# Two transformer blocks on one core: SBUF laid out anew, with stage boundaries and the routing reordered

## The chip, the core and the metric

The kernel runs on one core of one Trainium2 chip as a single program: TensorE (PE) multiplies matrices, VectorE (DVE), ScalarE (ACT) and GpSimd (POOL) do the rest, SyncE (SP) issues most DMA transfers. Everything on chip lives in SBUF (128 partitions; addresses below are offsets within a partition) or in the eight banks of PSUM, into which PE writes. The metric is the device time of one execution in microseconds (us); the median of three runs stands for the kernel.

## The reference

The input is 512 tokens of 1024 float32 values. Two layers of a first block are followed by one second block:

```python
for l in range(2):                              # first block
    h = rms_norm(x, attn_norm[l])
    proj = h @ w_in[l]                          # 13 parts: fox q k v f, diff q k v, dsa q k v, index q k w
    o = concat(fox_attention, diff_attention, dsa_attention)   # dsa: top 128 keys chosen by the index scores
    x = x + o @ w_out[l]
    gate, up = split(rms_norm(x, ffn_norm[l]) @ w_gate_up[l])  # 1024 -> 2 x 2816
    x = x + (silu(gate) * up) @ w_down[l]
proj = rms_norm_2(x, mix_norm_gain) @ w_in_2    # second block: q, k, v, u, two gates
merged = gate0 * (chunked_attention(q, k, v) @ wb[:512]) + gate1 * (s5_ssm_glu(u) @ wb[512:])
x = x + merged @ w_out_2
h = rms_norm_2(x, ffn_norm_gain_2)
x = x + moe(h)       # 4 groups of 4 experts, 1024 -> 256 -> 1024; the best group, 2 experts of it per token
```

## The kernel before

**Precision.** A float32 product is made of three reduced ones. `unit` fetches 4 KiB per partition of weights (`raw`, DMA issued by SP, L158), ACT rounds them to `hi` (L162), and DVE or POOL forms the rest `lo` (L164). An activation matrix is kept the same way, transposed, as `Th` and `Tl` (two tiles each, for k 0 to 3 and 4 to 7): `put_T` transposes one block of 128 tokens and 512 features on PE (L196), ACT copies it to Th (L199), DVE writes the rest to Tl (L200). The product is three matmuls: `mm3` (L174 to L176) moves weights against stationary activations, `mm3w` (L1139 to L1141) moves activations against stationary weights. In the profile `out<-moving,stationary` names the operands; s, f, t and o are the PSUM banks, two of each, s and f for accumulators.

**Order.** The program is written engine-free; a scheduler sets each engine's order from the order of the code, the buffers and their releases. Every tile that is reused waits for its last reader.

**Stages.** A norm is opened (`norm_open`), fed a block at a time (`norm_block`: DVE multiplies by the gain into `big`, L217, `put_T`, ACT sums squares, L219) and closed (`norm_close`, L223 to L226, gives the factor r per token, which is applied after the products). Each mixer closes the norm, then `project` makes the index, key and value part (4 accumulators over 8 k's); from these banks qk_norm (L289 to L297, its reciprocal root at L134 to L141), the v split (L372) and per block z, ix and iw (L575 to L577) read directly. A second projection follows, then attention in softmax passes: scores on PE, maximum m on DVE, exponential p on ACT (L428), halves pp on ACT and POOL (L433), transposed pt. Then the product with w_out feeds the FFN's norm. The FFN works column by column: gate and up by `mm3w` (t and o), then the down products by `mm3` (s and f) from the rounded hidden halves hh and hl.

**Second block.** u is projected for each of four token phases (slice r of stride 4). Its factor per phase, r4, is made by writing r to a DRAM row rd and reading it back in another order (L976, L978). `ssm` copies the banks out as um with it (L1409). The attention's and SSM's outputs are yA and yS; branch products and gates give `merged` (mh, ml), which w_out takes. In its last half each block's eight k's give 20 logits by `mm3` (96 matmuls of 20 columns over the four blocks); then lg (L1542), ranks, the list of slots, and a gather per expert from the normalised copy hd (stored at L1606 after normalisation on ACT, L1605). The gather buffers xe are zeroed first by POOL (L1680). Sixteen experts follow, each with six units of weights.

**Where things lie** (built addresses, KiB): hi 33.8 to 45.8, lo 45.8 to 57.8, Th and Tl of mixers and second block 57.8 to 90, yA and yS 108 to 138, hh and hl 108 to 160, the FFN's Th and Tl in a pool of their own (`home`) at 190 to 222, expert weights' spare hi and lo at 184 to 208.

## Time and profile before

| | us |
|---|---|
| median of 3 runs (1992.2, 2000.2, 2000.66) | 2000.2 |
| the profiled execution | 2000.87 |
| its span on the core | 1999.1 |
| PE busy in the span | 1852.3 |
| DVE, ACT, POOL busy | 1244.6, 871.2, 532.4 |

| stage | us from the span's start |
|---|---|
| load and first norm | 0 to 30 |
| mixer, FFN (layer 0) | 30 to 338, 338 to 720 |
| mixer, FFN (layer 1) | 733 to 1010, 1030 to 1406 |
| second block to w_out | 1407 to 1777 |
| routing, MoE, end | 1777 to 1812, to 1966, to 1999 |

The profiled execution took 1.8 us more than its span. "Busy" of PE counts pipelined matmuls whose records overlap, so a matmul's cost is read from start to start. The granted clock of PE is a share of full speed: 1.00 is 2.4 GHz, 0.50 is 1.2 GHz.

### The profile page before, as it was taken

How to read it: one execution, taken by the hardware profiler on the slowest of the kernel's cores; microseconds unless marked ns; L12 is line 12 of the kernel's file. 1: busy time of each engine (PE TensorE's matmuls, PEld its weight loads, DVE VectorE, ACT ScalarE, POOL GpSimd, SP SyncE). 2: the span in 40 equal slices, each digit the busy share in tenths (PEclk: the TensorE clock that was granted, in tenths of full speed). 3: DMA queues.
4: the chain of work that ended last, by engine and by line, in shares of the span. 5: the costliest groups of instructions: out<-in, count | busy, mean ns of one | idle time of the engine just before them, and what ended most of it. 6: DMA issues, size and time to landing. Idle time of an engine off the chain costs nothing.

```text
span 1999.1 us, 30880 instructions
## 1 busy us (share of the span) xinstructions
PE 1852.3 (93%) x11506; PEld 1552.9 (78%) x11506; DVE 1244.6 (62%) x2779; ACT 871.2 (44%) x1411; POOL 532.4 (27%) x452
## 2 busy tenths in 40 slices
PE   6998798999999999978999999999899989997994
PEld 5788687888888878867978888888788778886783
DVE  4789875433334458998776687534265465457994
ACT  4455564322122234555652222323234674345883
POOL 4476640000000045765300000000344640022321
PEclk8999899999999999999999999999899999988997
DMA  5244764333333242556744355332642455567993
GB/s 160 56 101 100 149 115 118 95 95 95 95 95 95 85 127 75 109 113 136 137 117 110 110 169 154 114 112 85 223 148 64 106 125 160 195 245 253 309 308 65
DMA packets 383890, 265.88 MB, mean 133 GB/s; under 512 B 163713, under 2 KB 344989, under 8 KB 383217
## 3 DMA queue, kind: packets, MB, share of 16 engines
q1 hardware_dynamic: 379120, 255.39, 46.3%
q0 software_dynamic: 4608, 8.40, 1.8%
q8 instruction: 93, 1.52, 0.3%
q14 instruction: 69, 0.56, 0.1%
HBM read 213.21 MB, written 26.26 MB: 120 GB/s over the span
## 4 chain that ended last, share of the span: by engine, by line
PE 65%; DVE 16%; DMA 10%; issue 4%; ACT 3%; POOL 2%; SPq 0%; POOLq 0%; ACTq 0%; DVEq 0%
PE f L174 5%; PE f L175 5%; PE f L176 5%; PE t L1139 4%; PE t L1140 4%; PE t L1141 4%; PE o L1139 4%; PE s L174 4%; PE o L1140 4%; PE o L1141 4%; PE s L175 4%; PE s L176 4%; DVE lo L164 2%; DVE m L608 2%; DVE work L609 2%
## 5 line engine op out<-in xcount | busy, mean ns | idle before, releaser
L162 ACT CAST hi<-raw 128x1024 fp32r<-128x1024 f32 (+2 forms) x330 | 334.2, 1017 | 681.7 <-PE f L176 233.1
L164 POOL TENSOR_TENSOR lo<-raw,hi 128x1024 fp32r<-128x1024 f32 (+1 forms) x89 | 205.7, 2316 | 673.7 <-ACT hi L162 673.5
L164 DVE TENSOR_TENSOR lo<-raw,hi 128x1024 fp32r<-128x1024 f32 (+1 forms) x241 | 287.2, 1200 | 146.1 <-ACT hi L162 135.3
L174 PE MATMUL f<-hi,Th 128*128 128x256 f32 (+2 forms) x800 | 257.4, 322 | 6.9 <-DVE vt L372 4.3
L175 PE MATMUL f<-lo,Th 128*128 128x256 f32 (+2 forms) x800 | 256.3, 320 | 0.5 <-POOL lo L164 0.5
L176 PE MATMUL f<-hi,Tl 128*128 128x256 f32 (+2 forms) x800 | 255.3, 319 | 0.3 <-DVE m L426 0.3
L174 PEld LDWEIGHTS f<-hi,Th 128*128 128x128 f32 x800 | 157.5, 197 | 17.4 <-issue 2.9
L175 PEld LDWEIGHTS f<-lo,Th 128*128 128x128 f32 x800 | 157.9, 197 | 8.7 <-POOL lo L164 1.0
L176 PEld LDWEIGHTS f<-hi,Tl 128*128 128x128 f32 x800 | 157.2, 197 | 8.7 <-DVE m L426 0.7
L1139 PE MATMUL t<-Th,hi 128*128 128x512 f32 x352 | 140.5, 399 | 0.0
L1140 PE MATMUL t<-Tl,hi 128*128 128x512 f32 x352 | 139.8, 397 | 0.0
L1141 PE MATMUL t<-Th,lo 128*128 128x512 f32 x352 | 139.6, 397 | 0.0
L1139 PE MATMUL o<-Th,hi 128*128 128x512 f32 x352 | 139.1, 395 | 0.0
L1141 PE MATMUL o<-Th,lo 128*128 128x512 f32 x352 | 138.9, 395 | 0.0
L1140 PE MATMUL o<-Tl,hi 128*128 128x512 f32 x352 | 138.9, 395 | 0.0
L174 PE MATMUL s<-hi,Th 128*128 128x512 f32 (+1 forms) x224 | 92.4, 413 | 18.2 <-ACT um L1409 8.5
L433 POOL TENSOR_TENSOR pp<-p,pp 128x384 f16<-128x384 f32 (+1 forms) x82 | 80.8, 991 | 90.8 <-ACT pp L432 74.4
L428 ACT ACTIVATE p<-p,m 128x384 f32<-128x384 f32 (+3 forms) x128 | 67.5, 557 | 68.1 <-DVE m L426 53.8
L175 PE MATMUL s<-lo,Th 128*128 128x512 f32 (+1 forms) x224 | 91.4, 408 | 3.2 <-POOL lo L164 3.2
L176 PE MATMUL s<-hi,Tl 128*128 128x512 f32 (+1 forms) x224 | 90.9, 406 | 0.0
L174 PE MATMUL f<-hi,hh 128*128 128x512 f32 x208 | 82.8, 398 | 2.7 <-ACT hh L1784 2.2
L176 PE MATMUL f<-hi,hl 128*128 128x512 f32 x208 | 82.6, 398 | 0.6 <-DVE hl L1785 0.6
(735 smaller groups left out, 4742.0 us busy)
## 6 DMA issues: line engine op xcount, KB each, us to landing
raw<-in_w_gate_up_dram SPq DMA_DIRECT2D x88, 512.0 KB, 3.9
raw<-in_w_in_dram SPq DMA_DIRECT2D x52, 512.0 KB, 4.0
raw<-in_w_down_dram SPq DMA_DIRECT2D x44, 512.0 KB, 3.7
raw<-in_w_e_down_dram SPq DMA_DIRECT2D x26, 512.0 KB, 8.3
raw<-in_w_e_gate_dram SPq DMA_DIRECT2D x50, 256.0 KB, 7.2
raw<-in_w_e_up_dram SPq DMA_DIRECT2D x50, 256.0 KB, 7.2
par<-par SPq DMA_DIRECT2D x4, 2304.0 KB, 11.5
raw<-in_w_in_dram SPq DMA_DIRECT2D x32, 256.0 KB, 3.2
```

Of the source, the lines that this page charges most:

```text
L162: nc.scalar.copy(hi, raw)
L164: low.tensor_tensor(out=lo, in0=raw, in1=hi.bitcast(F32), op=ALU.subtract)
L174: nc.tensor.matmul(out, l[0], r[0], start=start, stop=False)
L175: nc.tensor.matmul(out, l[0], r[1], start=False, stop=False)
L176: nc.tensor.matmul(out, l[1], r[0], start=False, stop=stop)
L428: nc.scalar.activation(p[:, at[qb]:at[qb] + (qb + 1) * P], src[qb], AF.Exp, bias=m[:, i:i + 1], scale=-1.0)
L433: nc.gpsimd.tensor_tensor(out=pp[:, o:2 * o], in0=p[:, :o], in1=pp[:, :o], op=ALU.subtract)
L608: nc.vector.max(m8, work[qb])
L609: nc.vector.match_replace(out=work[qb], in_to_replace=m8, in_values=work[qb], imm_value=TAKEN)
L1139: nc.tensor.matmul(out, w[0], r[0], start=start, stop=False)
L1140: nc.tensor.matmul(out, w[0], r[1], start=False, stop=False)
L1141: nc.tensor.matmul(out, w[1], r[0], start=False, stop=stop)
```

## The change

**Layout.** The pool of hi and lo now lies lowest (hi 16 to 28, lo 28 to 40), and above it eight slabs of 8 KiB, two sets of four (40 to 72 and 72 to 104). A norm's T takes one set: the FFN's set 1, the others' set 0. The set not in use serves as room: the mixer's softmax buffers (`KINDS`: s for p, p for pp, t for pt) and the relu of the index scores, yA and yS, um and U, the spare hi and lo of the experts. raw, big and constants lie above 104; hh and hl at 140 to 187, mh and ml at 172 to 204.

**Boundaries.** `norm_block` puts its transposes on a list, and `flush(n, 1)` runs them a block late; the last ones are flushed after the first four k's of the next stage's first product, in `project`, in the FFN's first column and in `logits`. `norm_close` follows that product. In the mixer's start every accumulator is copied out once (p0, in `big`), and qk_norm, v, z, ix and iw read p0. In the second block r4 is made from the broadcast row of r by a masked sum, and um is copied by ACT and DVE in turn.

**Routing.** `logits` takes the 40 columns of router weights (hi and lo side by side) as the stationary operand and moves T (384, then 128 tokens), then copies and transposes the result. hd is stored unnormalised, a block at a time during w_out, as is the output; r goes into the gates. The memsets are gone. Between the halves of w_out expert 0's gate and up units are fetched and split. hi and lo have 7 sets in place of 6; weights wait in 20 raw buffers by turns in place of 23, after a first few.

```diff
-SLOTS = {'p': 2, 'pp': 2, 'pt': 5}
...
-PRE = 15
+PRE = 7
...
-MORE_D, MORE_F = ('sp', 'ttpptt')
+KINDS, MORE_F = 'sssppptttttt', 'tttp'
...
+        self.ring = pool("ring", bufs=3)
+        self.hp = pool("hp", bufs=1)
+        self.cur = 0
...
+        self.rawp = pool("rawp", bufs=3)
+        self.bigp = pool("bigp", bufs=1)
...
-        hi = ring.tile([P, n], F32R, tag="hi", name="hi")
-        lo = ring.tile([P, n], F32R, tag="lo", name="lo")
+        hi, lo = (next(self.rings) if self.rings else self.parts_of(self.ring))(n)
...
+        return self.bigp.tile([P, NT, D], F32, tag="big", name="big", bufs=1)
+
+    def slab(self, k, dt=F32R, other=True):
+
+        return self.hp.tile([P, 4, S], dt, tag=f"T{self.cur ^ other}{k}", name=f"T{k}")
+
+    def new_T(self, other=False):
+        self.cur ^= other
+        return [[self.slab(2 * j + i, other=False) for i in range(2)] for j in range(2)]
...
-        self.put_T(n.T, n.big[:, tb, :], tb, h)
+        n.todo.append(lambda: self.put_T(n.T, n.big[:, tb, :], tb, h))
         nc.scalar.activation(self.junk, n.x[tb][:, hs], AF.Square, accum_out=n.ss[:, h, tb:tb + 1])
+
+    @staticmethod
+    def flush(n, left=0):
+
+        while len(n.todo) > left:
+            n.todo.pop(0)()
...
                 done([b.rearrange("p (t c) -> p t c", t=2) for b in banks])
             yield
 
-    def project(self, T, w, parts, order=range(KD // 2)):
+    def project(self, T, w, parts, sl=lambda tb: slice(tb * P, (tb + 1) * P), norm=None):
+
         acc = [self.acc() for _ in range(NT)]
         n = sum(n for _, n in parts)
-        for i, k2 in enumerate(order):
-            hi, lo = self.columns(w, (2 * k2, 2 * k2 + 1), parts)
-            for kk in range(2):
-                for tb in range(NT):
-                    self.mm3(acc[tb][:, :n], self.Tk(T, 2 * k2 + kk, slice(tb * P, (tb + 1) * P)), (hi[:, kk, :], lo[:, kk, :]), i == kk == 0, i == KD // 2 - 1 and kk == 1)
+        for h in range(2):
+            units = []
+            for k2 in (2 * h, 2 * h + 1):
+                hi, lo = self.columns(w, (2 * k2, 2 * k2 + 1), parts)
+                units += [(2 * k2 + kk, hi[:, kk, :], lo[:, kk, :]) for kk in range(2)]
+                if norm is None or h:
+                    for k, hi, lo in units:
+                        for tb in range(NT):
+                            self.mm3(acc[tb][:, :n], self.Tk(T, k, sl(tb)), (hi, lo), k == 0, k == KD - 1)
+                    units = []
+            for tb in range(NT):
+                for k, hi, lo in units:
+                    self.mm3(acc[tb][:, :n], self.Tk(T, k, sl(tb)), (hi, lo), k == 0, False)
+            if norm is not None and h == 0:
+                self.flush(norm)
         return acc
 
...
+                    self.flush(n, 1)
...
+        acc = self.project(T, w, [(SK, IW + 4 - SK), (FF, 6)], norm=n)
+        self.norm_close(n)
+        p0 = self.big()[:, :, 0:IW + 10 - SK]
+        for tb in range(NT):
+            r = rx[:, tb:tb + 1]
+            if tb % 2:
+                nc.vector.tensor_scalar(p0[:, tb, :], acc[tb][:, 0:IW + 10 - SK], r, None, op0=ALU.mult)
+            else:
+                nc.scalar.activation(p0[:, tb, :], acc[tb][:, 0:IW + 10 - SK], AF.Copy, scale=r)
...
+        room = [v[:, i * S:(i + 1) * S] for v in slabs[0:3] for i in range(4)]
         sqk = one.tile([P, NT, 7 * 64], F32, name="sqk")
-        r_sk = self.qk_norm(acc, 0, 1, 64, g_sk, sqk[:, :, 384:448], "sk", ex)
-        sv = self.v_parts(acc, SV - SK, 1, "sv", rx)
...
-        for tb in range(NT):
-            r = rx[:, tb:tb + 1]
-            nc.vector.scalar_tensor_tensor(z[:, tb, :], acc[tb][:, IW + 4 - SK:IW + 10 - SK], r, fb, op0=ALU.mult, op1=ALU.add)
-            nc.scalar.activation(ix[:, tb, :], acc[tb][:, IQ - SK:IW - SK], AF.Copy, scale=r)
-            nc.vector.tensor_scalar(iw[:, tb, :], acc[tb][:, IW - SK:IW - SK + 4], r, 0.5, op0=ALU.mult, op1=ALU.mult)
-        ixv = ix.rearrange("p t (h d) -> p t h d", h=5)
...
-                rl = self.att.tile([P, S], F32, tag="p", name="rl", bufs=SLOTS["p"])[:, :L]
+                rl = next(rls)[:, :L]
...
                         self.norm_block(following, tb, half)
+                        self.flush(following, 1)
...
+                        self.flush(n)
                     if c == 0:
+                        self.norm_close(n)
...
-        rd = self.dram.tile([S], F32, name="rd")
-        nc.sync.dma_start(out=rd.rearrange("(t p) -> p t", p=P), in_=rx)
-        r4 = self.tiny.tile([P, 4], F32, name="r4")
-        nc.sync.dma_start(out=r4, in_=rd.rearrange("(m r) -> m r", r=4))
...
-        yS = [(ys.tile([P, S], F32R, name=f"ysh{i}"), ys.tile([P, S], F32R, name=f"ysl{i}")) for i in range(4)]
+        pairs = lambda h, l: [(h[:, i, :], l[:, i, :]) for i in range(4)]
+        yS = pairs(self.slab(0), self.slab(2))
...
+                acc = self.project(T, w, [(1536, 512)], lambda r: slice(r, S, 4), n)
+                self.norm_close(n)
+                self.norm_row(n, self.raw_of(self.rawp)(S), self.upto)
+
+                r4, t4 = self.tiny.tile([P, 4], F32, name="r4"), self.raw_of(self.rawp)(S).rearrange("p (r m) -> p r m", r=4)
+                nc.vector.tensor_mul(t4, n.rB.rearrange("p (m r) -> p r m", r=4), self.ident[:, None, :].to_broadcast([P, 4, P]))
+                nc.vector.tensor_reduce(r4, t4, axis=AX.X, op=ALU.add)
...
+            self.hd = self.dram.tile([S, D], F32, name="hd")
             self.pre = self.ctx.enter_context(tc.tile_pool(name="pre", bufs=PRE))
+
+            sets = [[self.slab(k) for k in (j, j + 2)] for j in range(2)]
+            self.sets = [lambda n, h=h, l=l, i=i: [v[:, i:i + 2, :].rearrange("p a t -> p (a t)")[:, 0:n] for v in (h, l)] for h, l in sets for i in (0, 2)]
...
                     if half:
-                        for k in range(KD):
-                            self.mm3(self.logits[:, tb * 20:(tb + 1) * 20], self.Tk(n.T, k, slice(tb * P, (tb + 1) * P)), (self.rw[0][:, k, :], self.rw[1][:, k, :]), k == 0, k == KD - 1)
+                        nc.sync.dma_start(out=self.hd[tb * P:(tb + 1) * P, :], in_=n.big[:, tb, :])
+                        nc.sync.dma_start(out=out[tb * P:(tb + 1) * P, :], in_=x[tb])
+                    self.flush(n, 1)
                 return add
 
             for half in range(2):
                 self.accumulate(put(half), half, wo, [(k, 2) for k in range(0, KD, 2)], lambda k, t: (M[k][0][:, t], M[k][1][:, t]), half)
+                if half == 0:
+                    self.raws, self.rings = cycle([self.raw_of(self.pre)]), iter(self.sets)
+                    self.ahead = list(gate_up(self, 0))
+                    self.raws = self.rings = None
+            self.norm_close(n)
+            logits(self, n)
...
     for r in range(4):
-        nc.scalar.activation(um[:, :, r, :], acc[r].rearrange("p (g c) -> p g c", g=NG), AF.Copy, scale=r4[:, r:r + 1])
+        src = acc[r].rearrange("p (g c) -> p g c", g=NG)
+        if r % 2:
+            E.tensor_scalar(um[:, :, r, :], src, r4[:, r:r + 1], None, op0=ALU.mult)
+        else:
+            nc.scalar.activation(um[:, :, r, :], src, AF.Copy, scale=r4[:, r:r + 1])
...
-    self.logits = self.sm()
+
+    self.rw = c.tile([P, KD, 40], F32R, name="rwp")
+    nc.scalar.copy(self.rw[:, :, 0:20], raw)
+    nc.vector.tensor_sub(self.rw[:, :, 20:40], raw, self.rw[:, :, 0:20].bitcast(F32))
+    self.lb = self.sm()
+
+
+def logits(self, n):
+
+
+    nc = self.nc
+    ps = self.lb
+
+    def add(ks, c0, c1):
+        for k in ks:
+            hi, lo = self.Tk(n.T, k, slice(c0, c1))
+            mm = [(40, hi), (20, lo)]
+            for m, v in mm[::-1] if k == KD - 1 else mm:
+                nc.tensor.matmul(ps[0:m, c0:c1], self.rw[:, k, 0:m], v, start=k == 0 and m == 40, stop=k == KD - 1 and m == 40)
+
+    last = S - P
+    add(range(KD), 0, last)
+    add(range(4), last, S)
+    self.flush(n)
+    add(range(4, KD), last, S)
+    lT = self.raw_of(self.rawp)(S)
+    nc.scalar.copy(lT[0:40, 0:256], ps[0:40, 0:256])
+    nc.vector.tensor_copy(lT[0:40, 256:S], ps[0:40, 256:S])
+    ps = self.sm()
+    for tb in range(NT):
+        nc.tensor.transpose(ps[:, tb * 40:(tb + 1) * 40], lT[0:40, tb * P:(tb + 1) * P], self.ident[0:40, 0:40])
+    self.logits = ps[:, 0:NT * 40].rearrange("p (t c) -> p t c", t=NT)
 
...
-    for tb in range(NT):
-        E.scalar_tensor_tensor(lg[:, tb].rearrange("p g e -> p (g e)"), self.logits[:, tb * 20:(tb + 1) * 20], n.r[:, tb:tb + 1], self.rb, op0=ALU.mult, op1=ALU.add)
+    lf = lg.rearrange("p t g e -> p t (g e)")
+    E.tensor_copy(lf, self.logits[:, :, 20:40])
+    E.tensor_add(lf, lf, self.logits[:, :, 0:20])
+    E.tensor_mul(lf, lf, n.r[:, :, None].to_broadcast([P, NT, 20]))
+    E.tensor_add(lf, lf, self.rb[:, None, :].to_broadcast([P, NT, 20]))
...
-        for tb in range(NT):
-            nc.scalar.activation(n.big[:, tb, :], n.big[:, tb, :], AF.Copy, scale=n.r[:, tb:tb + 1])
-            nc.sync.dma_start(out=hd[tb * P:(tb + 1) * P, :], in_=n.big[:, tb, :])
-        self.store_x(x, out)
...
+        self.rings = cycle([ring, sets[0], sets[1], ring, sets[2], sets[3], ring])
+        self.raws = chain([self.raw_of(self.pre)] * (PRE - 4), cycle([self.raw_of(self.pre)] * 4 + [self.raw_of(self.rawp)] * 3 + [self.raw_of(self.more)] * MORE + [lambda n, v=v: v[:, 0:n] for v in x[XR:] + room] + [self.raw_of(self.pre)] * (PRE - 4)))
...
-        for v in xe:
-            nc.gpsimd.memset(v, 0.0)
...
-    for k, w in gate_up(self, e):
+    ahead, self.ahead = self.ahead, None
+    for k, w in ahead or gate_up(self, e):
         self.mm3(ps, (xh[:, k], xl[:, k]), w, k == 0, k == KD - 1)
```

PE at the first mixer's end and the FFN's start, before (big is the normed block, t and o banks; L196 transposes):

```order
L176 MATMUL f<-hi,Tl 128x512
L196 MATMUL t<-ident,big 128x128 x4
L196 MATMUL o<-ident,big 128x128 x4
L196 MATMUL t<-ident,big 128x128 x4
L196 MATMUL o<-ident,big 128x128 x4
L1139 MATMUL t<-Th,hi 128x512
L1140 MATMUL t<-Tl,hi 128x512
L1141 MATMUL t<-Th,lo 128x512
```

The same place after (T_4380 and T_4382 are Th and Tl for k 0 to 3, T_4381 is Th for k 4 to 7; L202 transposes):

```order
L180 MATMUL f<-hi,T_2613 128x512
L202 MATMUL t<-ident,big 128x128 x4
L202 MATMUL o<-ident,big 128x128 x4
L1182 MATMUL o<-T_4380,hi 128x512
L1183 MATMUL o<-T_4382,hi 128x512
L1184 MATMUL o<-T_4380,lo 128x512
...
L202 MATMUL t<-ident,big 128x128 x4
L1182 MATMUL t<-T_4380,hi 128x512
...
L202 MATMUL o<-ident,big 128x128 x4
L248 MATMUL t<-big,ones 128x128 x2
L1182 MATMUL o<-T_4381,hi 128x512
```

Two of the four groups of transposes now stand behind 12 and 24 gate or up products of the first four k's.

SP's queue at the second block's start, before (rd and r are the factor on its way, bias and rel the attention's, raw weights):

```order
L976 DMA rd<-n_14336 128x4x1
L997 DMA rel<-rr 8x639
L145 DMA gk_15141<-in_k_gain_dram 128x64
L158 DMA raw<-in_w_in_dram 128x2x512 x3
L978 DMA r_14739<-rd 128x4
L1076 DMA bias<-rel 128x512 x2
L158 DMA raw<-in_w_in_dram 128x2x512 x4
```

The same place after:

```order
L147 DMA gk_14785<-in_k_gain_dram 128x64
L164 DMA raw<-in_w_in_dram 128x2x512
L1029 DMA rel<-rr 8x639
L164 DMA raw<-in_w_in_dram 128x2x512
L1108 DMA bias<-rel 128x512 x2
L164 DMA raw<-in_w_in_dram 128x2x512 x3
```

rd and its read are gone; weights no longer stand behind them.

PE at the end of w_out, after (mh and ml are `merged`, rwp the router weights, T_1731x the norm's T, raw the copied logits). Before, the 96 products `o<-rwh,Th` and their like of 20 columns stand here, with the last t and o transposes among them:

```order
L180 MATMUL f<-hi,ml_16849 128x512
L1594 MATMUL o<-T_17310,rwp 40x384
L1594 MATMUL o<-T_17312,rwp 20x384
...
L202 MATMUL t<-ident,big 128x128 x4
L1594 MATMUL o<-T_17311,rwp 40x384
L202 MATMUL o<-ident,big 128x128 x4
L1594 MATMUL o<-T_17313,rwp 20x384
...
L1594 MATMUL o<-T_17310,rwp 40x128
...
L1606 MATMUL t<-ident,raw 128x40 x4
```

The long products of the first three blocks go ahead of the last block's transposes; 16 short ones and four transposes follow.

## Rows read from the trace of the kernel before

**Rows 1.** The page's busy time by engine (share of the span) and instructions:

```profile
PE 1852.3 (93%) x11506; PEld 1552.9 (78%) x11506; DVE 1244.6 (62%) x2779; ACT 871.2 (44%) x1411; POOL 532.4 (27%) x452
```

**Rows 2.** Stretches: length, busy of each engine (instructions), PE's clock, DMA share, GB/s:

```profile
345.00:700.00 355.00, 355.00 (x1537) 285.80 (x1537) 134.63 (x150) 96.94 (x121) 0.00 (x0) 1.00 0.32 92
130.00:250.00 120.00, 101.99 (x1165) 92.98 (x1164) 107.14 (x315) 70.20 (x138) 82.93 (x81) 0.91 0.60 126
1860.00:1965.00 105.00, 102.98 (x535) 83.75 (x536) 103.27 (x129) 86.61 (x118) 32.21 (x17) 1.00 0.88 281
```

**Rows 3.** PE's timeline, FFN gate and up (start, us, instruction):

```profile
399.85 0.39 PE L1139 MATMUL o<-Th,hi 128*128 128x512 f32 x1
...
406.85 0.39 PE L1139 MATMUL t<-Th,hi 128*128 128x512 f32 x1
```

**Rows 4.** PE's timeline, branch products of the second block:

```profile
1693.69 0.39 PE L1139 MATMUL f<-yah,hi 128*128 128x512 f32 x1
...
1695.79 0.39 PE L1139 MATMUL s<-Th,hi 128*128 128x512 f32 x1
...
1701.25 0.39 PE L1139 MATMUL f<-yah,hi 128*128 128x512 f32 x1
```

**Rows 5.** The page's group of one FFN product (count, busy, mean ns):

```profile
L1139 PE MATMUL t<-Th,hi 128*128 128x512 f32 x352 | 140.5, 399 | 0.0
```

**Rows 6.** PE's timeline, FFN down products:

```profile
499.85 0.40 PE L174 MATMUL f<-hi,hh 128*128 128x512 f32 x1
...
502.18 0.39 PE L175 MATMUL f<-lo,hh 128*128 128x512 f32 x1
```

**Rows 7.** The chain in order at the second block's start (start, us):

```profile
1412.75 19.51 DMA rd<-n
...
1438.36 0.70 ACT um L1409
```

**Rows 8.** PE's waits (us, times, longest): 1428 to 1448; 730 to 742; 1014 to 1026:

```profile
PE s L174 <- ACT um L1409: 8.5, 1, 8.5
...
PE s L174 <- DVE rs L139: 4.0, 1, 4.0
...
PE t L196 <- DVE big L217: 1.7, 2, 1.1
PE o L196 <- DVE big L217: 1.4, 1, 1.4
```

**Rows 9.** Stretches of PE: length, busy (instructions), clock, DMA share, GB/s:

```profile
1439.10:1444.60 5.50, 5.50 (x13) 0.50 0.60 182
...
338.48:342.74 4.26, 4.26 (x12) 0.50 0.62 203
```

**Rows 10.** The chain in order in the routing (start, us):

```profile
1777.22 0.23 PE f L176
...
1786.07 0.98 PE o L196 x4
...
1788.32 8.00 DMA hd<-big
...
1802.11 7.74 DMA big<-hd,sia
```

**Rows 11.** DVE's timeline in the routing (start, us, instruction, idle before):

```profile
1783.53 3.38 DVE L164 TENSOR_TENSOR lo<-raw,hi 128x1024 fp32r<-128x1024 f32 x1
...
1787.69 0.69 DVE L200 TENSOR_TENSOR Tl<-o,Th 128x512 fp32r<-128x512 f32 x1
1795.18 0.68 DVE L1542 SCALAR_TENSOR_TENSOR lg<-o,n,rb 128x20 f32<-128x20 f32 x4 [6.80 <-PE o L176]
```

**Rows 12.** The chain in the MoE, its longest piece (start, us):

```profile
1862.51 10.36 DMA raw<-in_w_e_gate_dram
```

**Rows 13.** A stretch with DVE: length, busy (instructions), clock, DMA share, GB/s:

```profile
1760.00:1780.00 20.00, 9.60 (x13) 0.99 0.33 126
```

**Rows 14.** The page's group of POOL's softmax halves (count, busy, mean ns):

```profile
L433 POOL TENSOR_TENSOR pp<-p,pp 128x384 f16<-128x384 f32 (+1 forms) x82 | 80.8, 991 | 90.8 <-ACT pp L432 74.4
```

166 lines of the change are left out of this document (80 added, 86 removed).

## The prediction

> **What bounds the kernel now.** I read the page's totals first, then busy time by stretch, then waits and single rows at the stage boundaries. TensorE is busy 1852.3 of 1999.1 us [rows 1]. By stretch: in the FFN PE is busy in all 355.00 of 355 us at clock 1.00, so there only a shorter matmul helps. In the mixer DVE is the fuller one (107.14 of 120 us, PE 101.99). In the MoE PE (102.98) and DVE (103.27) both fill 105 us and the DMA share is 0.88, so three resources end nearly together [rows 2]. Three questions follow: does a matmul get shorter, which waits at boundaries go, and does the MoE pass an earlier start on to the end.
>
> **Operands at low addresses: −13.1 us.** The measure is the spacing of matmul starts, since records overlap. In the FFN's gate and up products T (Th, Tl) moves, from 190 to 222 KiB: 30 matmuls from 399.85 to 406.85, 233.3 ns each [rows 3]. In the second block's branch products operation and weights are the same for two moving operands: yah and yal at 124 to 138 KiB take 2.10 us for 9 (1693.69 to 1695.79, 233.3 ns), T at 58 to 90 KiB takes 5.46 us for 24 (to 1701.25, 227.5 ns) [rows 4]. So I read 5.8 ns as the price of the high address. One FFN product, t<-Th,hi, has 352 matmuls [rows 5]; with t and o and three products each there are 2112, and 2112 × 5.8 = 12.3 us. As built, the changed kernel puts hi and lo at 16 to 40 KiB and the FFN's T at 72 to 104; its last 14 KiB lie above what the fast row covers, so I take 12.0. The 192 products of yA and yS, now in slabs, add 192 × 5.8 = 1.1. The down products gain nothing: low weights moving against hh and hl above 108 KiB are spaced 233 ns already (10 from 499.85 to 502.18) [rows 6], and hh and hl go higher still. PE is saturated in the FFN, so nothing hides this term.
>
> Against it speaks the Trainium skill, "SBUF — State Buffer", section "SBUF: two separate sides": PE reads through ports of its own and waits for nobody, and the page gives a matmul no dependence on the offset. By it the sum would be 13.1 us smaller. The pair of rows with equal weights does not agree with it.
>
> **Second block's start: −9.5.** The factor r goes to DRAM element by element and comes back as r4. The write rd<-n stands 19.51 us in the chain [rows 7], and PE waits 8.5 us for the first um [rows 8]. Then PE runs 5.50 us at clock 0.50, its lower level of 1.2 GHz [rows 9], and half of that, 2.7, is lost. The change forms r4 on PE and DVE while the projection still runs, and takes both DMAs out of SP's queue, where weight loads stood behind the read. All four accumulator banks are full when the projection ends, so the next one still waits for an eviction: ACT's took 0.70 [rows 7], with the handover about 1.0. Gain 8.5 + 2.7 − 1.0 = 10.2 if the clock stays up, 7.5 if it falls again. I take 9.5, near the first, since the pause left is shorter than the 1.4 us ones below. Late next would be the loads of the SSM's parameters, in SP's queue as before; no row shows them late, so they are costed at nothing.
>
> **Mixer starts: −4.0.** In each of the two mixers the second projection waits 4.0 us for rs L139 [rows 8], the end of qk_norm, which reads the bank. Now each bank is copied out once, two by ACT and two by DVE; a copy is the 0.70 above, so 1.0 of wait remains, and (4.0 − 1.0) × 2 = 6.0. In the built order DVE does sk's norm right behind, but no bank waits for that. DVE is the fuller engine later in the stage [rows 2], and a gain ahead of it holds only as far as its own chain starts earlier. The rotation and the index scores do move up. Range 0 to 6.0; I take 4.0, nearer to the full gain because the start of DVE's chain hangs on the same copies.
>
> **Mixer to FFN: −3.1.** At each of the two boundaries PE waits 1.7 and 1.4 us for DVE's product with the gain (big L217), ahead of the last transposes [rows 8]: 6.2 together. At the first one it then runs 4.26 us at clock 0.50 [rows 9], 2.1 of it lost. Now two of the four groups of transposes stand behind 12 and 24 gate and up products (the order above), 12 × 0.2275 = 2.7 us of cover; the other two wait as before. So half of the waits goes, 3.1, and I leave the clock as it is. Range 1 to 8.3.
>
> **Routing and MoE: −6.5.** The last product of w_out starts at 1777.22 and the gather is issued at 1802.11, 24.9 us later. Between them the last o transposes come only at 1786.07, and beside that runs the store hd<-big of 8.00 us with POOL's memset behind it [rows 10]. DVE is held there by a split lo of 3.38 us; from the last Tl (1787.69) it is 7.5 us to lg (1795.18), all of it logits products, and 6.9 from lg to the gather [rows 11]. The change stores hd a block at a time, drops the memsets and transposes the logits. Behind the last o come about 8 products of 128 columns (0.2 each, as the short ones had: 36 in 7.5), a copy of 0.7, four transposes of at most 1.0 together, three more DVE steps of 0.2: 1.6 + 0.7 + 1.0 + 0.6 = 3.9, against 7.5. So 3.6 goes, and 7.0 if the split gets out of the way too. The gather (7.74) [rows 10] stays. Whether the MoE passes it on is open: its chain holds weight loads of 10.36 us [rows 12]. For it speaks the hole in the transfers ahead (share 0.33 from 1760 to 1780) [rows 13], into which hd and the output now go; and expert 0's four units are split before the MoE begins, which takes four of DVE's and ACT's from a full stretch. Against it: four units fewer, 2 MB, stand ahead of the stores in SP's queue, some 7 us at the MoE's 281 GB/s [rows 2]. Range 0 (all eaten) to −13 (7.0 and the head start); I take −6.5, the middle, since the rows for and against weigh alike.
>
> **Sum.** 13.1 + 9.5 + 4.0 + 3.1 + 6.5 = 36.2. The profiled execution took 2000.87 us (span 1999.1) and the median of the three runs is 2000.2, so the two agree. 2000.9 − 36.2 = 1964.7, or 1965.
>
> **Rivals.** (A) The address does nothing, and the kind of product makes the spacing; this is the page's rule above as a mechanism of this kernel. 13.1 us less gain, 1978. For it: low weights moving in the down products are spaced 233 ns. Against: the branch pair. (B) The MoE is set by its bytes, and the routing's gain is given back: 1965 + 6.5 = 1971. For it the 0.88 share and the 2 MB, against it the hole. (C) Both, and the mixers end on DVE's chain and the FFN boundaries give nothing: 1965 + 13.1 + 6.5 + 7.1 = 1992, within half a per cent, which is about the least that a measurement of this kernel can tell from no change. (D) Slower: the softmax buffers p, pp and pt are now quarters of three slabs in the mixers; if a slab came free only as a whole, one pass would run at a time. A pass then adds at least POOL's half pp, 991 ns, 82 times [rows 14]: 81 us, 2046. It decides from 36.2 / 82 = 0.44 us a pass. Against it: today's T is written by block while other blocks of the same tile are read, and there are no fewer buffers of each kind. That the change misses its target is left out for the layout, since the built addresses are low, and the order has moved as shown.
>
> **How the numbers follow.** Forecast 0.69, A 0.10, B 0.12, C 0.05, D 0.04. Faster by over 0.5% 0.91, within 0.05, slower 0.04. The forecast's bounds toward more gain (12.3, 10.2, 6.0, 8.3 and 13 in place of 12.0, 9.5, 4.0, 3.1 and 6.5: 14.7 more if all came at once) give 1950. A with B, 1965 + 13.1 + 6.5, gives 1985. Outside lie C and D, 0.09.
>
> **What would show it.** Gate and up products spaced 227 to 228 ns in both FFNs, some 12 us shorter together; at 233, A. No wait above 1.5 us at the second block's start and no 4.0 in the mixers. The gather issued 18 to 21 us after w_out's last product. If it is, and the MoE is longer by as much, B. Softmax passes longer by over 0.4 us each: D. A wait that no term names, above all one for a slab, would make the sum wrong.

## The result

The changed kernel takes 1965.72 us (median of four runs, 1964.43 to 1966.12) where the kernel before, run beside it, takes 2000.43: a ratio of 0.983, 95% interval 0.980 to 0.986. The forecast was 1965.0. The total came out right; the table shows that its parts did not. A stage runs from one event on PE to the next, in the profiled execution (1999.1 us of span before, 1962.6 after); PV is the product of the softmax with the values.

| stage (from, to) | before | after | difference |
|---|---|---|---|
| start, first PV of mixer 0 | 125.1 | 118.2 | −6.9 |
| to its last PV | 188.5 | 175.8 | −12.7 |
| to the first gate product | 24.3 | 25.9 | +1.6 |
| FFN 0, to its last down product | 374.7 | 368.9 | −5.8 |
| to the first PV of mixer 1 | 106.5 | 97.0 | −9.5 |
| to its last PV | 177.4 | 179.0 | +1.6 |
| to the first gate product | 26.4 | 25.7 | −0.7 |
| FFN 1 | 383.6 | 381.8 | −1.8 |
| second block, to its first PV | 177.2 | 164.9 | −12.3 |
| its attention, first to last PV | 86.0 | 108.8 | **+22.8** |
| to the first product of w_out | 59.2 | 55.2 | −4.0 |
| w_out | 48.2 | 47.4 | −0.8 |
| end of w_out to the end | 222.0 | 214.0 | −8.0 |

One stage became longer by as much as two thirds of the whole gain, and nobody had asked for that. Some neighbouring rows have to be read together, since the same event cuts the work in another place after the change. Of the products of 512 columns, mixer 0's attention holds 45 (67 before) and the stretch behind it 82 (60); mixer 1's 45 (53) and 83 (75); the second block's attention 236 (219) and the stretch behind it 238 (256). And 22 projection products of 256 columns moved from mixer 1's start into its attention. A product of 512 columns takes 0.23 us, one of 256 columns 0.12.

The rows of after, in the order of the groups of before:

The page's totals (busy time, share of the span, instructions); they answer [rows 1]:

```profile
PE 1823.8 (93%) x11446; PEld 1534.7 (78%) x11446; DVE 1258.1 (64%) x2769; ACT 861.5 (44%) x1382; POOL 531.7 (27%) x444
```

PE's timeline in the FFN, gate and up products (start, length, us); 30 products lie between the two rows, which answer [rows 3]:

```profile
381.46 0.39 PE L1184 MATMUL o<-T,lo 128*128 128x512 f32 x1
...
388.26 0.39 PE L1184 MATMUL t<-T,lo 128*128 128x512 f32 x1
```

The same view for the down products, which answer [rows 6]; again 30 products apart:

```profile
479.89 0.40 PE L179 MATMUL s<-lo,hh 128*128 128x512 f32 x1
...
486.89 0.40 PE L179 MATMUL f<-lo,hh 128*128 128x512 f32 x1
```

Gate and up products now start every 6.80 / 30 = 226.7 ns (233.3 before), FFN 0's down products still every 7.00 / 30 = 233.3.

PE's waits (us in total, times, longest) in the second block, 1372 to 1537 and then 1537 to 1646; the first row answers [rows 8]:

```profile
PE o L1472 <- ACT big L1512: 1.0, 1, 1.0
...
PE o L476 <- DMA at<-at: 14.1, 8, 4.0
```

The wait of 8.5 us for um is gone, no wait there is above 1.0. In the attention behind it eight waits of 14.1 us stand at the PV product, for a name that the kernel before did not have: at<-at. Before, the same view of the same stage had three such waits:

```profile
PE o L452 <- DMA pt<-pp: 3.1, 3, 1.7
```

Stretches of the changed kernel (length; busy time of PE, PEld, DVE, ACT, POOL with instructions; PE's clock; DMA share; GB/s): the second block's start, its attention, and the whole end from w_out on:

```profile
1372.30:1537.20 164.90, 163.92 (x864) 140.31 (x862) 85.49 (x132) 71.23 (x103) 86.68 (x52) 1.00 0.40 137
...
1537.00:1646.00 109.00, 88.38 (x710) 70.87 (x710) 46.45 (x124) 62.20 (x94) 33.68 (x31) 0.89 0.47 106
...
1748.50:1962.60 214.10, 167.65 (x924) 133.78 (x922) 166.45 (x261) 131.08 (x179) 62.96 (x38) 0.91 0.80 254
```

The second block's start is full (163.92 of 164.90 us, clock 1.00). Its attention is not: PE idles for 20.6 of 109 us, and its clock falls to 0.89.

The routing, PE's and POOL's timelines; they answer [rows 10, 11]:

```profile
1748.48 0.39 PE L180 MATMUL f<-hi,ml 128*128 128x512 f32 x1
1748.71 1.56 PE L1594 MATMUL o<-T,rwp 128*40 128x384 f32 x8
...
1763.40 1.25 POOL L1827 DMA_INDIRECT big<-hd,sia  x1 [9.43 <-DVE rest L1720]
```

From the last product of w_out to the gather it is 14.9 us, 24.9 before.

### The profile page after: what moved, and what is told of

It reads as the page before. It is cut to its first block, busy times and chain, and to the rows that moved or that the text cites. A ratio compares the mean times of both kernels' runs of the same rounds, so it can differ in the third digit from the quotient of the medians.

```text
span 1962.6 us, 30674 instructions
## 1 busy us (share of the span) xinstructions
PE 1823.8 (93%) x11446; PEld 1534.7 (78%) x11446; DVE 1258.1 (64%) x2769; ACT 861.5 (44%) x1382; POOL 531.7 (27%) x444
## 5 line engine op out<-in xcount | busy, mean ns | idle before, releaser
L178 PE MATMUL f<-hi,T 128*128 128x256 f32 (+2 forms) x764 | 243.6, 319 | 3.4 <-DVE rs L142 3.0
L179 PE MATMUL f<-lo,T 128*128 128x256 f32 (+2 forms) x764 | 241.4, 316 | 0.7 <-POOL lo L168 0.7
L180 PE MATMUL f<-hi,T 128*128 128x256 f32 (+2 forms) x764 | 239.6, 314 | 0.0
L178 PEld LDWEIGHTS f<-hi,T 128*128 128x128 f32 x764 | 150.2, 197 | 11.3 <-issue 3.7
L179 PEld LDWEIGHTS f<-lo,T 128*128 128x128 f32 x764 | 150.1, 196 | 7.3 <-POOL lo L168 1.1
L180 PEld LDWEIGHTS f<-hi,T 128*128 128x128 f32 x764 | 149.4, 196 | 6.2 <-issue 0.2
L1182 PE MATMUL o<-T,hi 128*128 128x512 f32 x352 | 137.8, 392 | 0.0
L1182 PE MATMUL t<-T,hi 128*128 128x512 f32 x352 | 137.8, 391 | 0.0
L1183 PE MATMUL o<-T,hi 128*128 128x512 f32 x352 | 137.5, 391 | 0.0
L1184 PE MATMUL o<-T,lo 128*128 128x512 f32 x352 | 137.5, 391 | 0.0
L1183 PE MATMUL t<-T,hi 128*128 128x512 f32 x352 | 137.1, 389 | 0.0
L1184 PE MATMUL t<-T,lo 128*128 128x512 f32 x352 | 137.0, 389 | 0.0
L178 PE MATMUL s<-hi,hh 128*128 128x512 f32 x190 | 76.1, 401 | 1.7 <-ACT big L1882 1.3
L1183 PEld LDWEIGHTS o<-T,hi 128*128 128x128 f32 x352 | 66.5, 189 | 13.8
L1182 PEld LDWEIGHTS o<-T,hi 128*128 128x128 f32 x352 | 66.5, 189 | 13.7
```

What stands on the lines that cost most here:

```text
L178: nc.tensor.matmul(out, l[0], r[0], start=start, stop=False)
L179: nc.tensor.matmul(out, l[0], r[1], start=False, stop=False)
L180: nc.tensor.matmul(out, l[1], r[0], start=False, stop=stop)
L1182: nc.tensor.matmul(out, w[0], r[0], start=start, stop=False)
L1183: nc.tensor.matmul(out, w[0], r[1], start=False, stop=False)
L1184: nc.tensor.matmul(out, w[1], r[0], start=False, stop=stop)
```

## Experiments

Each run is the changed kernel with one edit unless something else is said. "Undone" costs are against 1965.7. The kernel before, run beside each group of them, took 1998.5 to 2002.4, and stages that an edit leaves alone differ by some 2 us, so a cost of 4 us or less says little.

### The new wait in the second block's attention

`buffers` hands out softmax tiles from three generators, made in a loop over "spt". The inner one names `kind`, but reads it only when it is first asked for a tile; by then the loop is over and `kind` is "t" for all three. In the mixers this never shows, as there the tiles come from slabs. In the second block all three kinds come from one set of five `at` tiles: p, pp and pt of a pass take three of five. Theory: this is the 14.1 us. Rival: the order of the fill work, or the low scratch addresses. The edit binds `kind` early, 2 + 2 + 5 tiles as the table says:

```diff
-        self.ps, self.pps, self.pts = (cycle(sets[kind]) if sets else (of(kind) for _ in count()) for kind in "spt")
+        self.ps, self.pps, self.pts = [cycle(sets[kind]) if sets else (lambda kind: (of(kind) for _ in count()))(kind) for kind in "spt"]
```

> The changed kernel with one difference: in the second block's attention p, pp and pt get tiles of their own (2, 2 and 5) instead of sharing five. The trace of after shows PE waiting there 14.1 us for the DMA transposes (3.1 before) and DVE 11.5 us for them, and the stretch from the second block's first product to the first of w_out 328.5 us against 322.0 before, although the 8.5 us wait for um is gone. Theory (the five shared buffers make the new waits): this stretch falls to about 310 to 315 us, PE's wait for the transposes to about 3, and the time to about 1950 (1945 to 1957). Rival (the order of the fill work or the low scratch addresses make them): stretch and waits stay, 1962 to 1968.

1943.51 us (1941.35 to 1948.41), ratio 0.972 (0.969 to 0.975), below the 1945 to 1957 that the theory gave. The attention takes 81.7 us (108.8), and the stretch behind it, to which 21 products went back, 58.4 (55.2). Its stretch, and what PE still waits for at the PV product:

```profile
1537.00:1619.00 82.00, 74.85 (x679) 61.67 (x678) 45.56 (x118) 59.84 (x92) 34.34 (x31) 0.98 0.67 138
...
PE o L476 <- DMA at<-ap: 3.9, 3, 3.3
```

The waits fell from 14.1 to 3.9, PE's idle time from 20.6 to 7.2, and the clock rose from 0.89 to 0.98. The sum of the edit, 22.2 us, is more than the idle time: with fewer and shorter pauses the clock also stayed up. The theory holds: a slip of one line hid 22 us of gain.

### Where the sets lie

The two shared sets of T go behind constants, raw and big, to 74 to 138 KiB; everything else keeps its order.

```diff
-        self.hp = pool("hp", bufs=1)
         self.const = pool("const", bufs=1)
         self.rawp = pool("rawp", bufs=3)
         self.bigp = pool("bigp", bufs=1)
+        self.hp = pool("hp", bufs=1)
```

> The changed kernel with the eight slabs allocated above the constants, raw and big, so that set 0 starts near 76 KiB and the FFN's T (set 1) near 108 KiB; hi and lo stay low and no instruction is added or removed. Theory (the address of the moving operand sets the spacing): gate and up products return from 227 to 233 ns, each FFN is 5 to 7 us longer, the mixers and the second block are little changed, and the time is 1976 to 1982. Rival (the kind of product, or the order, makes the spacing): 227 ns and 1963 to 1969 as in the changed kernel.

1985.59 us (1981.39 to 1987.57), 19.9 more, above the 1976 to 1982 expected. FFN 0 takes 375.4 us (368.9), FFN 1 389.4 (381.8). 30 gate and up products:

```profile
381.43 0.40 PE L1183 MATMUL o<-T,hi 128*128 128x512 f32 x1
...
388.47 0.39 PE L1183 MATMUL t<-T,hi 128*128 128x512 f32 x1
```

7.04 / 30 = 234.7 ns. So where the sets lie decides the spacing, as predicted. But as built, FFN 0's T lies at 106 to 138 KiB here and FFN 1's at 74 to 106 (in the changed kernel at 72 to 104 and at 40 to 72; the two FFNs use different sets). T at 58 to 90 KiB was fast in the kernel before [rows 4]; gate and up products with T at 74 to 90 KiB came out slow here, 234 ns. Height alone can't be the rule. So the dispute was measured by itself, in a kernel with nothing but such products in PE's order of the FFN, over 11 heights of each operand from 16 to 192 KiB (zeros, other engines idle), and then again with real numbers, alone, beside loads, and beside loads with ACT and DVE splitting them (7 × 3 heights).

> A program of its own: fp32r products of 512 columns on zeros, 12 in a row for each pair of 11 moving and 11 stationary offsets from 16 to 192 KiB, and a result of zeros; nothing of the reference is computed. Theory (the moving operand's address decides, with an edge between 90 and 106 KiB): spacing 227 ns for moving offsets below the edge and 233 above it, whatever the stationary offset. Second theory (either operand above the edge costs it, as hh and hl suggest: 228 ns in the second FFN before, 234 after they moved up): 227 only where both are low. Rival (no dependence on the offset): one spacing for all pairs.

> A program of its own: a copy of the input's first 128 rows and fp32r products of 512 columns in the order of the FFN's (two moving tiles 16 KiB apart, two stationary ones 12 KiB apart), for 7 moving and 3 stationary offsets, first with the other engines idle, then beside weight loads, then beside loads, ACT's hi and DVE's lo; nothing of the reference is computed. The run with zeros and idle engines showed 226.7 ns for every pair of offsets, so the offset alone does not make 233. Theory A (it needs real data or the alternation of tiles): 233 above the edge already in the first part. Theory B (it needs other traffic on SBUF): 227 everywhere in the first part, 233 for high offsets in the second or third. Rival (neither; something else that moves with the pools): 227 in all three.

Both grids: 226.6 to 226.7 ns for every pair and in every part. Neither height, nor data, nor traffic, nor the other engines make a product slow there. So both theories of height fell. Where that happens, look for what the runs kept constant: here all tiles stood at multiples of 1 KiB from one another. In the kernels they don't. Set against the addresses in the built programs, the starts of the 512-column products of the kernel before and of the changed one sort by one number, the moving operand's byte address minus the stationary one's, modulo 256:

| difference | where | median ns | mean ns |
|---|---|---|---|
| 0 | before: T of the mixers and the second block | 227 | 229.4 |
| 64 | before: FFN 1 down (mean 229.1), w_out (231.8) | 229 | 229.8 |
| 128 | before: FFN 0 down, yS | 232 | 232.5 |
| 192 | before: gate, up, yA | 233 | 233.3 |
| 0 | after: T of every stage, yA, yS | 227 | 227.7 |
| 160 | after: FFN 1 down, w_out | 234 | 234.2 |
| 224 | after: FFN 0 down | 232.5 | 233.3 |

The third grid holds the height and shifts each operand by 0 to 256 bytes.

```python
SH = (0, 4, 8, 16, 24, 32, 48, 64)             # floats
...
th = t[:, 6144 + m + (i % 4) * 512: 6144 + m + (i % 4) * 512 + 512]      # moving, m in SH
hi = t[:, s + i * 128 + k0 * 1024: s + i * 128 + k0 * 1024 + 128]        # stationary, s in SH
```

> A kernel with nothing but 1,536 fp32r products of 512 columns, back to back, in the order of the feed-forward block ((hi,Th), (hi,Tl), (lo,Th)), on real numbers, all tiles below 60 KiB; it computes nothing of the reference. Both moving tiles are shifted together, and both stationary tiles together, by 0, 16, 32, 64, 96, 128, 192 or 256 bytes from a multiple of 256: 64 pairs, 24 products each. In the two grids before, every tile stood at the same offset modulo 128, and every pair ran at 226.6 to 226.7 ns. Theory D (what sets the spacing is whether the moving and the stationary operand start at the same byte offset modulo 128, and the high tiles of the kernel before were merely ones that did not: 96 against 32): 226.7 ns where the two shifts are equal modulo 128, 233 to 234 ns where they are not, so that 0 with 128 and 256, and 64 with 192, are fast and 0 with 32 or 96 slow. Rival (each operand's own alignment matters, not the relation): whole rows or whole columns are slow. Rival (something else that moves with the pools): 226.7 in all 64.

Mean ns from start to start, 24 products a cell (a pause in the first cell left out); a column is the moving operand's shift in bytes, a row the stationary one's:

```
            0     16     32     64     96    128    192    256
   0    226.7  231.4  232.7  228.7  233.9  233.5  233.0  227.6
  16    226.7  230.1  228.3  232.1  230.4  233.3  231.8  226.7
  32    233.1  227.0  228.3  233.4  229.3  233.9  233.8  233.3
  64    233.4  234.7  233.1  227.0  233.4  229.3  232.3  233.3
  96    233.9  233.2  233.0  233.0  227.0  233.4  233.1  233.9
 128    233.5  233.3  233.8  233.6  233.1  227.7  229.6  232.7
 192    229.0  231.2  233.7  232.3  234.0  233.4  227.5  229.6
 256    227.2  231.4  233.5  228.7  233.9  233.5  233.0  227.5
```

The expected rule was nearly right: agreement counts, but modulo 256, not 128 (0 against 128 is slow, 233.5). On the diagonal, and between 0 and 256, it is 226.7 to 228.3 ns (16 with 16 excepted: 230.1); where the moving operand stands 64 above the stationary one (columns over rows: 64 over 0 and 256, 96 over 32, 128 over 64, 192 over 128, 0 and 256 over 192) 228.7 to 229.6; for the other pairs of multiples of 32 232.3 to 234.0. Agreement is not the whole rule: with the shift of 16 bytes the pairs with the moving operand 16 below the stationary one are as fast (0 and 256 over 16, 16 over 32: 226.7 to 227.0), and the others, 228.3 to 234.7, follow no order that I can name. The three levels are those of the table above, the 229.1 of FFN 1's down products included; w_out's 231.8 before is the one entry that the grid does not give.

Does it carry the kernel's time? Two runs cross height with alignment: the sets low but shifted by 32 bytes, and the sets high (73 to 137 KiB) with two constants moved behind them, so that they agree with the weights modulo 256.

```diff
+        pool("pad", bufs=1).tile([P, 8], F32, name="pad")     # low, shifted
         self.hp = pool("hp", bufs=1)
```

```diff
         self.bigp = pool("bigp", bufs=1)
+        self.hp = pool("hp", bufs=1)                            # high, aligned
+        self.const2 = pool("const2", bufs=1)
...
-        self.nhalf = c.tile([P, NT], F32, name="nhalf")
+        self.nhalf = self.const2.tile([P, NT], F32, name="nhalf")
...
-        self.rope = c.tile([P, NT, 24], F32, name="rope")
+        self.rope = self.const2.tile([P, NT, 24], F32, name="rope")
```

> The changed kernel with one unused 32-byte tile ahead of the shared activation sets: they stay at the low addresses (40.2 to 104.2 KiB), but start 160 bytes past a multiple of 256 while the weight parts stay at 128. Theory D, now by the grid (fast only where moving and stationary operand agree modulo 256, half of the loss where the moving one stands 64 above, else slow): the gate and up products go back from 226.8 to 233 ns although every address is low, 2112 of them cost 13 us, the mixers' starts and the second block's products some 4 to 7 more as in the run with the high sets (1985.6, FFN stages +6.5 and +7.6): 1979 to 1987 us. Theory of the prediction (low operand addresses): nothing changes, 1963 to 1968 us and 227 ns.

> The changed kernel with the shared sets behind the constants, the raw ring and the big buffer, at 73 to 137 KiB, as in the run that cost 20 us, but with two constants of 416 bytes moved behind them, so that the sets start 128 bytes past a multiple of 256, as the weight parts do. Theory D (agreement modulo 256): gate and up products at 227 ns, 1963 to 1969 us as the changed kernel, that is all 20 us of the run with high sets come back without moving the sets down. Theory of the prediction (low addresses): 234 ns and 1983 to 1989 us.

Low and shifted: 1980.26 us (1979.20 to 1986.59), FFNs 374.5 and 387.7 us. High and aligned: 1964.11 (1962.08 to 1965.79), FFNs 369.2 and 381.8. The 32 bytes also moved hh and hl, to differences of 192 and 128 from the weights (224 and 160 in the changed kernel), which made FFN 1's down products 232.4 ns (234.1), 0.9 us shorter in all. The FFN's timelines, 30 products apart, first low and shifted:

```profile
381.57 0.39 PE L1184 MATMUL o<-T,hi 128*128 128x512 f32 x1
...
388.57 0.39 PE L1184 MATMUL t<-T,hi 128*128 128x512 f32 x1
```

and high and aligned:

```profile
381.57 0.39 PE L1185 MATMUL o<-T,lo 128*128 128x512 f32 x1
...
388.37 0.39 PE L1185 MATMUL t<-T,lo 128*128 128x512 f32 x1
```

233.3 and 226.7 ns. Alignment gives and takes the whole effect on these products, 33 KiB of height nothing. In the changed kernel the sets agree with hi and lo because they now stand directly behind the ring of hi and lo, whose 24 KiB are a multiple of 256 bytes; no edit aimed at that.

### What the transposes behind the next products give

```diff
-        n.todo.append(lambda: self.put_T(n.T, n.big[:, tb, :], tb, h))
+        self.put_T(n.T, n.big[:, tb, :], tb, h)
```

> The changed kernel with put_T run at once in norm_block, so that no transposes are left for the next stage; all else is kept. The prediction put 3.1 us on the two mixer to FFN boundaries, while the traces show them unchanged (50.6 us before, 51.5 us after, from the last value product to the first gate product). Theory A (the delay of the transposes gives the gain at the starts of the mixers and of the second block, where stages begin sooner): 1972 to 1980, with most of it lost ahead of the first attention scores. Theory B (the single copy out of the banks gives that gain and the delay little): 1963 to 1970.

1988.22 us (1986.80 to 1989.18), 22.5 more, above both ranges. The first boundary to the FFN costs 2.4 of it, the second 0.1, and the FFNs, without transposes of the boundary in them, give 3.1 back. The mixers' starts, where Theory A had most of it, cost 0.6 and 1.6, mixer 1's attention 3.6; the second block's start costs 12.0, and the end 6.6, of which 4.2 stand ahead of the gather (19.1 us after w_out's last product, 14.9 in the changed kernel). PE's waits at the second block's start, and in the routing:

```profile
PE o L1511 <- DVE St L1503: 4.7, 2, 3.9
PE o L1472 <- DVE T L1454: 4.1, 1, 4.1
...
PE o L202 <- DVE big L223: 3.3, 1, 3.3
```

So the edit that I priced at the two boundaries pays most where I had it down for nothing.

### r4 through DRAM again

```diff
+        self.norm_close(n)
+        rd = self.dram.tile([S], F32, name="rd")
+        nc.sync.dma_start(out=rd.rearrange("(t p) -> p t", p=P), in_=rx)
+        r4 = self.tiny.tile([P, 4], F32, name="r4")
+        nc.sync.dma_start(out=r4, in_=rd.rearrange("(m r) -> m r", r=4))
...
-                self.norm_close(n)
...
-                nc.vector.tensor_reduce(r4, t4, axis=AX.X, op=ALU.add)
```

> The changed kernel with r4 made as before: the norm is closed ahead of the projection, r goes to a DRAM row and comes back in another order; the late transposes, the two-engine copy of um and all else stay. The run without the delay already lost 12 us between the second FFN's last product and the second block's attention, with r4 still made on the chip. Theory of the prediction (the round trip is worth 9.5 us by itself): the wait of about 8 us for um returns and the time is 1973 to 1979. Rival (the delay of the transposes makes the gain there and the trip hides behind it): 1963 to 1969, no such wait.

1975.58 us (1971.84 to 1979.19), 9.9 more, of which the second block's start takes 7.0 (171.9 us, 164.9). The wait for the first um is back there, with 4.9 us of its old 8.5:

```profile
PE s L178 <- ACT T L1456: 4.9, 1, 4.9
```

### The mixers' starts read the banks again

The single copy p0 is taken out; sk's norm, v, z, ix and iw read the accumulators as before.

```diff
-        p0 = self.big()[:, :, 0:IW + 10 - SK]
...
+        r_sk = self.qk_norm(acc, 0, 1, 64, g_sk, sqk[:, :, 384:448], "sk", ex)
+        sv = self.v_parts(acc, SV - SK, 1, "sv", rx)
+        ix = self.big()[:, :, 0:5 * 64]
```

> The changed kernel with the mixers' first evictions as before: qk_norm, v, z, ix and iw read the accumulator banks (ix now lies in big); the late transposes stay. In the trace of after the first value product of a mixer comes 6.9 and 9.5 us earlier than before, 16.4 together, where the prediction put 4.0 (0 to 6.0). Theory (the single copy gives most of it): 10 to 16 us longer, 1976 to 1982, and PE's wait of 4.0 us for rs is back in both mixers. Rival (it comes from the late transposes, of which the run without them gave back only some 2 us there, or from the buffers): 1965 to 1971.

1978.41 us (1976.41 to 1980.71), 12.7 more; mixer 0's start 125.2 us (118.2), mixer 1's 108.6 (97.0), together 18.6, of which the second block's attention and the stretch behind it, still short of buffers, give 3.3 back. PE's waits in mixer 1's start and two of its slices of 10 us:

```profile
PE s L178 <- DVE rs L141: 4.0, 1, 4.0
PE f L178 <- DVE vt L398: 3.0, 1, 3.0
...
714.30:724.30 10.00, 5.98 (x20) 4.68 (x20) 8.79 (x39) 5.06 (x18) 7.07 (x9) 0.83 0.46 134
...
764.30:774.30 10.00, 7.05 (x38) 6.87 (x37) 10.00 (x27) 3.34 (x5) 6.68 (x4) 0.67 0.21 53
```

Some 48 us behind the wait for rs stands a second one for vt, at the products of 256 columns, and the clock falls twice (0.83, 0.67). In the changed kernel no slice of that stage is below 1.00, though a wait of about the same length stands at those products:

```profile
PE f L178 <- DVE rs L142: 3.0, 1, 3.0
```

### hd and the output stored after the lists

```diff
-                    if half:
-                        nc.sync.dma_start(out=self.hd[tb * P:(tb + 1) * P, :], in_=n.big[:, tb, :])
-                        nc.sync.dma_start(out=out[tb * P:(tb + 1) * P, :], in_=x[tb])
...
+        for tb in range(NT):
+            nc.sync.dma_start(out=self.hd[tb * P:(tb + 1) * P, :], in_=n.big[:, tb, :])
+        self.store_x(x, out)
```

> The changed kernel with hd and the output stored after the routing's lists, as before, instead of a block at a time during w_out; still unnormalised and without memsets. Theory (the early store takes part in the routing's gain, since the gather waits for hd): the gather comes 3 to 8 us later and the time is 1968 to 1974. Rival (the chain of logits and lists sets the gather, the store hides beside it): 1964 to 1967.

1966.91 us (1962.91 to 1968.48): no difference that can be measured, and the gather is again issued 14.9 us after w_out's last product. The early store does not set the gather.

### Both findings together

Early binding, and pads of 224, 160, 96 and 128 bytes ahead of hh and hl of either FFN, of the merged branches and of the experts' buffers, so that all of them agree with the weights modulo 256.

```diff
+            st.enter_context(self.tc.tile_pool(name=f"pad{l}", bufs=1)).tile([P, (56, 40)[l]], F32, name="pad")
             hid = st.enter_context(self.tc.tile_pool(name=f"hid{l}", bufs=12))
...
+            st2.enter_context(self.tc.tile_pool(name="padm", bufs=1, side="right")).tile([P, 24], F32, name="pad")
...
+        pool("pade", 1).tile([P, 32], F32, name="pad")
```

> The changed kernel with the early binding of the attention's buffers (1943.5 us in its own run) and pads of 224, 160, 96 and 128 bytes ahead of the hidden activations of both feed-forward blocks, of the merged branches and of the experts' buffers, so that the stationary operands of the down products and of w_out agree with the weight parts modulo 256 (both 128) where they stood at 160 and 224 (0 in the experts). Theory D: down products 233.3 and 234.1 to 227 ns, 1056 x 6.7 = 7.1 us; w_out 192 x 7 = 1.3 us; the experts 0 to 2 us: 1932 to 1938 us, faster than every kernel here. Rival (these products are held by the weights' arrival or by their additions, not by their operands' addresses): 1941 to 1946 us.

1936.77 us (1932.77 to 1938.12), ratio 0.968 (0.967 to 0.970): the fastest kernel here. FFN 0 takes 365.8 us (369.1 with the early binding alone), FFN 1 378.3 (382.0), w_out 46.0 (47.3), 8.3 together; from w_out's end to the end it is 215.7 us (214.4), so the experts gave nothing. Down products, 30 apart:

```profile
480.06 0.39 PE L179 MATMUL s<-lo,hh 128*128 128x512 f32 x1
...
486.86 0.39 PE L179 MATMUL f<-lo,hh 128*128 128x512 f32 x1
```

6.80 / 30 = 226.7 ns, 233.3 in the changed kernel. So the additions and the weights' arrival don't hold these products.

## Why the prediction was right, and where it was not

The total was right by luck, because misses of both signs cancelled: the mixers and the deferred transposes gave more than their terms, and a wait that no term names took 22 back. With the buffers bound as the table says, the same forecast would have been 22 us too slow.

**Operand addresses, −13.1.** The effect exists and its size was read well: gate and up products went from 233.3 to 226.8 ns, 2112 × 6.5 = 13.7. The mechanism was wrong. The step that failed is "5.8 ns as the price of the high address": in the pair of [rows 4] yah and T differ in height, but also in alignment (192 and 0 from the weights, modulo 256), and I took height for the cause without a row that varied it alone. The Trainium skill's page that I set against it ("SBUF — State Buffer", section "SBUF: two separate sides") gives no dependence on the offset; for height the grids agree with it (226.6 to 226.7 ns from 16 to 192 KiB), and of the two operands' relation it says nothing. With the right rule the down products are no zero term either: their difference went from 64 to 160 in FFN 1 (229.1 to 234.1 ns, 528 × 5.0 = 2.6 us lost) and from 128 to 224 in FFN 0 (0.4). 13.7 − 3.0 would leave 10.7; the two FFNs gained 7.6, and the 3.1 between them are the transposes that now stand inside the FFNs: the run without the delay gives 3.1 back. Rival A, that the address does nothing, is refuted as far as the layout goes.

**Second block's start, −9.5.** It gained 12.3. Putting r4 back costs 7.0 there, putting the transposes back 12.0: the two overlap, and either alone would have left a wait of 4 to 5 us. The term's mechanism held; that the deferral works on the same wait was missing.

**Mixer starts, −4.0.** 16.4 us in the two starts, 18.6 by the run without the copy. The step that failed is the price. The waits alone gave 7.7, more than the 6.0 that I gave as the most: PE's idle time fell from 21.4 to 17.5 us in mixer 0's start and from 10.5 to 6.7 in mixer 1's. The clock, of which I had counted a fall for the second block, I left out here: for the same 582 products PE was busy 103.7 us in mixer 0's start before (clock 0.93) and 100.7 after (0.96). In mixer 1's it went like this, first before, then after:

```profile
712.60:819.00 106.40, 95.91 (x582) 85.11 (x580) 79.72 (x223) 46.63 (x95) 58.87 (x53) 0.97 0.33 86
...
688.80:785.80 97.00, 90.27 (x562) 79.75 (x560) 77.59 (x199) 40.99 (x78) 56.20 (x49) 1.00 0.34 93
```

Of these 5.6 us, 2.6 are no gain but the 22 products of 0.12 us that now run behind the first PV; the rest goes with the clock. The wait for vt that follows (3.3 in mixer 1 before) is no part of the gain, since 3.0 us for rs stand in its place after.

**Mixer to FFN, −3.1.** The rows say +1.6 and −0.7, but 22 and 8 more products of 512 columns run there, 5.0 and 1.8 us, and 8 transposes fewer in each. PE's idle time in the two stretches fell from 4.7 and 4.0 us to 2.8 and 2.8, 3.1 together; in the run without the delay they are 3.6 and 3.9, so 1.9 of the 3.1 are the delay's. The first stretch, before and after:

```profile
313.60:338.00 24.40, 19.73 (x109) 15.51 (x105) 19.34 (x35) 13.67 (x28) 0.23 (x1) 0.96 0.33 98
...
294.00:320.00 26.00, 23.24 (x121) 18.63 (x117) 17.66 (x31) 13.28 (x27) 0.00 (x0) 0.99 0.40 116
```

So the term came out about as forecast, with 2.0 us of waits for big L223 left at the first boundary (3.1 before). What it did not have is the same edit's 12.0 at the second block's start and 4.2 to 6.6 at the end.

**Routing and MoE, −6.5.** 8.0 from w_out's end to the end. The gather is issued 10.0 us earlier, more than the 3.6 to 7.0 that I gave; 2 us of it go in the experts, where the DMA share over the whole end is 0.80 (0.76 before). Rival B, that the MoE eats all of it, is refuted. The early hd store has no part in it; 4.2 of the gather's 10.0 come from the deferred transposes. The rest lies with the logits' new form, the absent memsets and expert 0's early units, which were not tried apart.

**Rival D and what it missed.** Softmax buffers were the right thing to fear. I looked for it in the mixers' slabs and counted kinds in the table, 2 + 2 + 5; the built program has five `at` tiles. The names in the built allocation would have shown it before any run.

**Open.** Mixer 0's attention became 12.7 us shorter (188.5 to 175.8), which no term names. 5.0 of it are the 22 products that moved behind it; the other 7.7 have no cause here. PE's busy time there fell by 8, those 5.0 among them, and DVE's waits for PE at fqk from 5.7 to 1.3 us. Sets high, transposes at once, r4 through DRAM, no single copy: each of these runs left it at 176.0 to 177.4, so none of them alone makes it. The softmax buffers in the slabs (3, 3 and 6 in the first passes for 3, 3 and 5, then 3, 4 and 9 for 2, 4 and 9) weren't tried; against them speaks that mixer 1's attention, which got the same, gained nothing (177.4 to 179.0). The undone costs don't add up to the gain either (19.9 + 22.5 + 9.9 + 12.7 = 65 against 34.7 + 22.2 = 57); where two edits work on one wait, as at the second block's start, they can't.

## What to carry to other kernels

Where a matmul is slower with one buffer than with another, compare the whole address of both operands, not the part that the layout is about, and test with the smallest shift that changes one of them. After a change of pools count the buffers that were built, by name. Before two stretches are compared, count the work in each: an event that is moved takes work from one stage to the next. A wait in PE is worth its length and what the clock loses after it, and a deferral pays at the boundary with the longest chain behind it, which need not be the one that shows the wait.

## What the runs showed of the hardware

An fp32r product of 512 columns starts 226.7 ns after the one before when its moving and its stationary operand begin at the same byte offset modulo 256, 229 ns when the moving one stands 64 bytes above, and 232 to 234 at other multiples of 32 bytes (third grid, and the table of the two kernels; single cells that agree took up to 228.3, and 230.1 at 16 with 16). Pairs that stand 16 bytes apart took from 226.7 to 231.4. It is 3% of PE's time in a stage that PE fills. With operands that agree, height between 16 and 192 KiB, the data, the DMA's writes and the other engines' work at the same time made no difference of 0.2 ns (first and second grid). Why it is so, no run here shows.
